# A one-core hybrid attention layer on Trainium2: opening loads cut in two, one more tile turned by VectorE, and a written order planned anew

## Chip, core and metric

The kernel runs on one core of one Trainium2 chip. The metric is the time of one execution in device microseconds (us), the median of several runs. A profiled execution has its own time and its own span, from the first to the last instruction.

## The reference, cut to what matters

One decoder layer on x of 2048 tokens by 1024 channels, all in float32:

```
h = rms_norm(x, norm_w);  proj = h @ w_in              # 1024 -> 2816 columns
rq, rk, rv, rg, sq, sk, sv, sg = split(proj)
ro = retention(rotary(rq), rotary(rk), rv)             # 4 heads, chunks of 128 tokens, a state carried on
ro = group_norm(ro) * ret_norm_w * silu(rg)
so = sliding_window_attention(sq, sk, sv, sinks, rel_bias) * silu(sg)   # 8 heads, window 128
return x + concat(ro, so) @ w_out                      # 1024 -> 1024
```

## The kernel before, in words

**Products.** The four large products (the projection in three groups of columns, 512, 384 and 512 wide, then the output projection, 512 wide) are made as Strassen products: seven products of blocks take the place of eight. For each of them, and for each of eight pairs of 128-token chunks, one product block is 12 matmuls of 512 (or 384) columns: 4 steps over the inner dimension, times 3 passes. The three passes are there because every float32 operand is split in a high part (`hi`, a rounded copy, made by ScalarE as a rule) and a low part (`lo`, the rest, made by VectorE): `xh*wh`, `xh*wl`, `xl*wh`. One group of columns has 56 such blocks.

**Small matmuls between them.** The sliding window needs 8 blocks `logits` (128 small matmuls each) and 8 blocks `values` (144 each); the retention needs 9 blocks `step` (up to 128 each); 16 single transposes turn keys (`turn k`). Of the 16 retention outputs that have been gated, those whose chunk is in `TURNED["gated"]` are turned by VectorE (a transpose of 32 by 32 blocks, a store to DRAM and four loads of 64 KB that put the blocks in place); the others take four transposes on TensorE and a copy by ScalarE. Before, 11 chunks are in the list and 5 are not (2, 7, 9, 12, 13).

**The order.** Every operation is entered into a `Program` with its engines and their costs, its buffers and a due time. `emit` then simulates the engines and writes the operations out, always the one that could start first by its costs, with the due time as tie-break and as the order of the queues. What it writes is the order of each engine on the chip; waits there are by semaphores. So a change of a due time (the tables `SHIFT` by label, `GROUPS` by label and stretch of 28 units, `SINGLE` by the operation's number) moves operations among others and changes no arithmetic. All plain loads and stores are issued by SyncE (SP) in one order.

**Instruction transfers.** TensorE's instructions are taken by the planner to come in pieces of 256 (`PIECE`), the next one asked for 320 instructions ahead (`ASKED`) and there `LONG` us later. An operation that would come to a border of pieces sooner is held back in the plan, so that others go first:

```
def late(o, s, occ):
    b, wait = border, 0.0
    while b <= place + o.many:
        a = b - ASKED
        at = s + (a - place) / o.many * occ if a >= place else asked.get(b, -LONG)
        wait = max(wait, at + LONG - s - (b - place) / o.many * occ)
        b += PIECE
    return wait
```

**The opening.** TensorE first runs ten warming matmuls on a constant. SP loads in turn a 256 KB tile of the first weights (`w`) and one of the first rows (`xfirst`, four chunks side by side), four of each. For inner step k=0, both 256-column halves of x are made high by ScalarE or VectorE, and w is scaled by the norm's weight and made high by ScalarE in one instruction (`part` with `split`). The first 48 matmuls go over the four chunks in turn, pass by pass for k below 3 (`products`, `passes`).

Of the kernel before, what the change touches and what calls it, by code (L numbers as in the profile page):

```python
# [40 lines left out]
NCH = S // P  # L41
# [22 lines left out]
SHARE = {"x": 25, "raw": 102, "acc": 73, "wr": 29, "wh": 16, "att": 27, "ret": 37, "rin": 87, "gate": 43, "mix": 73, "norm": 10, "res": 6, "turned": 3, "vn": 5, "first": 5, "block": 3, "rest": 6, "split": 53}  # L64

AHEAD_OF = {"x": 5.31, "wh": 14.22, "att": 30.46}

AHEAD, SPARE, SPARED = 13.889, 5, ("raw", "wr")

# [276 lines left out]
TURN = (1.9635, 2.7, 1.35)  # L346

GROUP = 28.0
GROUPS = {("scale k", 5): -0.35, ("load xk", 1): -0.74, ("mixed", 5): 0.86, ("load vn", 2): 1.11, ("load w", 0): 0.37}
SINGLE = {378: 2.98, 1033: 2.32, 910: -1.82, 395: 4.73, 18: -0.56, 25: 0.49, 394: -4.94, 1384: 4.33, 31: -0.91, 437: -1.09, 30: -2.54, 381: 2.45, 38: 0.49, 393: 0.51, 17: -0.02, 32: 0.37, 37: 4.06, 388: 2.37, 384: -1.41, 16: -1.27, 380: 0.9, 379: 3.45}  # L350

ACCUM = (1.25, 4.0, 0.1)

QUARTERS_IN = (1.05, 2.8, 1.6)

# [82 lines left out]
def layer(ctx, tc, xt, xfirst, xtok, nw, w_in, w_rn, qkw, sinks, biasg, rope, decays, dmask, gpow, w_out, out):  # L438
# [43 lines left out]
    def given(ap):  # L482
        return Buf(ap=ap)
# [42 lines left out]
    def f(t):  # L526
        return t.bitcast(F32)
# [61 lines left out]
    def split(raw, n, due, share, name, scale=None, quarters=False, labels=None):  # L589

        labels = labels or ("hi " + name, "lo " + name)
        hi, lo = kb(name, share, F32R), kb(name, share, F32R)
        of = (lambda t: t.rearrange("p (a k s) -> p k a s", a=4, s=32)) if quarters else (lambda t: t[:, :n])
        to = (lambda t: t.rearrange("p (k a s) -> p k a s", a=4, s=32)) if quarters else (lambda t: t[:, :n])
        if scale is None:
            op(
                {"A": act(n)}, lambda e: e.activation(to(hi()), of(raw()), AF.Copy), [raw], [hi], due,
                label=labels[0], also=(lo,),
            )
            op(  # L600
                both(n),
                lambda e: e.tensor_tensor(to(lo()), of(raw()), f(to(hi())), ALU.subtract),
                [raw, hi], [lo], due, label=labels[1],
            )
# [14 lines left out]
        return hi, lo  # L619
# [21 lines left out]
    def weights(src, c0, n, scale, base, seq):  # L641


        W = {m: [None] * 4 for m in range(1, 8)}
        at = {m: base + seq.first[m] for m in W}
        col, cols = scale

        def raw(q, i, due):
            t = kb("w", "wr")
            k, c = 4 * (q // 2) + i, c0 + q % 2 * n  # L650
            load(
                t, given(src[k * P : (k + 1) * P, c : c + n]), due - 3, n // 2, lambda t: t[:, :n],
                label="load first" if base == q == 0 else None,
            )
            return t

        def by(k):
            return (col, k) if k < cols else None

        def part(m, i, t, scale=None):  # L660
# [102 lines left out]
    def opening():  # L763

        made = []
        for k in range(KT // 2):
            t, hi, lo = kb("x", "raw"), kb("x", "x", F32R), kb("x", "x", F32R)

            load(t, given(xfirst[k]), -4.95 + 0.1 * k, label="load first")
            parts = []  # L770
            for i in range(2):
                c, due = slice(i * 256, (i + 1) * 256), -2.0 + 0.1 * k + 0.01 * i
                h, l = (Part(t, lambda t, c=c: t[:, c]) for t in (hi, lo))
                op(
                    {"A": act(256), "V": dve(256)} if k == 0 else {"A": act(256)},
                    lambda e, t=t, h=h, c=c: e.activation(h(), t()[:, c], AF.Copy) if e is A else e.tensor_copy(h(), t()[:, c]),
                    [t], [h], due, label="first hi", also=(hi, lo),
                )
                op(
                    both(256), lambda e, t=t, h=h, l=l, c=c: e.tensor_tensor(l(), t()[:, c], f(h()), ALU.subtract),  # L780
                    [t, h], [l], due, label="first lo", also=(hi, lo),
                )
                parts.append((h, l))
            made.append((hi, lo, parts))
        return made
# [4 lines left out]
    def products(B, W, n, base, seq, sink, plus=None, opening=None):  # L790
# [4 lines left out]
        def passes(m, acc, xh, xl, cols, k, d, goes_on, parts, which):  # L795


            wh, wl = W[m][k]
# [981 lines left out]
```

## Time and profile before

| | |
|---|---|
| median of 3 runs | 661.98 us (661.77 to 662.56) |
| the profiled execution's own time | 661.52 us |
| its span | 659.7 us |
| busy share: TensorE, VectorE, ScalarE, GpSimd | 99%, 87%, 71%, 7% |
| granted TensorE clock, mean | 0.999 |

In the profile PE is TensorE's matmuls, PEld its weight loads, DVE VectorE, ACT ScalarE, POOL GpSimd, SP SyncE; a q behind a name is that engine's sequencer. All instructions of this kernel have one line (434, a helper), so that groups are told apart by the tiles: `acc<-w,x` is a product block, `m<-ks,qT` logits, `m<-pT,vn` values, `m<-ident,ro` and `m<-ident,go` the turning of a gated tile. A row's busy time of matmuls is modelled at its end; the distance from one start to the next is the safer figure.

### The profile page before, as it was taken

The numbers are of one execution on the slowest core, as the hardware profiler recorded it, in microseconds if no ns is written. First come the engines' busy times: TensorE is split into PE (matmuls) and PEld (weight loads), VectorE is DVE, ScalarE is ACT, GpSimd is POOL, SyncE is SP. The second block draws the span as 40 slices with busy tenths as digits, with TensorE's granted clock in tenths as the row PEclk, the third lists the DMA queues.
The fourth block names the chain that finished last, engine by engine and source line by source line (L and its number), as shares of the span: only waits on it lengthen the run. The fifth ranks groups of instructions, "written<-read, shape, count | busy, mean of one in ns | idle before, by whom it ended". The sixth has DMA issues, their size and how long they took to land.

```text
span 659.7 us, 16248 instructions
## 1 busy us (share of the span) xinstructions
PE 654.7 (99%) x5930; PEld 561.2 (85%) x5930; DVE 574.0 (87%) x1328; ACT 469.1 (71%) x1141; POOL 43.5 (7%) x71
## 2 busy tenths in 40 slices
PE   9999999999999999999999999999999999999998
PEld 7888888888999999998888887888788888888886
DVE  5999987888689989899998999999999999974542
ACT  6774789667589778597999799898999765553000
POOL 0000000023300000000000000000000111133320
PEclk9999999999999999999999999999999999999999
DMA  9966399989598989999999989789999995179872
GB/s 317 386 231 239 112 327 313 320 264 325 122 237 259 255 232 275 342 300 302 278 233 275 259 272 289 211 268 245 260 287 257 181 284 135 40 138 205 192 160 97
DMA packets 152705, 160.34 MB, mean 243 GB/s; under 512 B 62000, under 2 KB 95152, under 8 KB 152624
## 3 DMA queue, kind: packets, MB, share of 16 engines
q1 hardware_dynamic: 147872, 150.90, 77.3%
q0 software_dynamic: 4608, 8.39, 8.1%
q8 instruction: 47, 0.77, 0.5%
q14 instruction: 34, 0.28, 0.1%
q10 hardware_dynamic: 144, 0.00, 0.0%
HBM read 97.32 MB, written 49.35 MB: 222 GB/s over the span
## 4 chain that ended last, share of the span: by engine, by line
PE 99%; issue 0%; DVE 0%; POOLq 0%
PE acc L434 88%; PE m L434 11%; DVE t L434 0%; POOLq L434 0%
## 5 line engine op out<-in xcount | busy, mean ns | idle before, releaser
L434 PE MATMUL acc<-w,x 128*128 128x512 f32 (+1 forms) x2700 | 586.5, 377 | 1.0 <-issue 1.0
L434 PEld LDWEIGHTS acc<-w,x 128*128 128x128 f32 x2700 | 493.9, 188 | 84.8 <-issue 4.8
L434 DVE TENSOR_TENSOR x<-x 128x512 fp32r<-128x512 f32 (+2 forms) x213 | 139.3, 681 | 11.5 <-ACT x L434 8.9
L434 ACT ACTIVATE x<-x 128x512 fp32r<-128x512 f32 (+1 forms) x180 | 106.7, 620 | 36.7 <-DVE x L434 16.4
L434 DVE TENSOR_TENSOR w<-w 128x512 fp32r<-128x512 f32 (+3 forms) x96 | 61.6, 666 | 3.9 <-ACT w L434 3.9
L434 ACT ACTIVATE lg<-lg,nm 128x160 f32<-128x160 f32 x128 | 53.0, 419 | 2.9 <-DVE nm L434 2.9
L434 DVE TENSOR_TENSOR s<-acc,s 128x512 f32<-128x512 f32 (+1 forms) x64 | 42.0, 657 | 13.8 <-PE acc L434 13.5
L434 DVE SCALAR_TENSOR_TENSOR w<-w,nw_sb 128x512 fp32r<-128x512 f32 (+3 forms) x72 | 49.8, 711 | 4.4 <-ACT w L434 3.0
L434 ACT ACTIVATE w<-w 128x512 fp32r<-128x512 f32 (+1 forms) x72 | 40.7, 603 | 13.0 <-DVE x L434 5.8
L434 DVE CUSTOM_DVE_ANT_0 lg<-m,bias,nsnk 128x160 f32<-128x160 f32 x128 | 39.8, 388 | 0.5 <-PE m L434 0.5
L434 DVE TENSOR_TENSOR t<-acc,t 128x512 f32<-128x512 f32 (+2 forms) x33 | 21.1, 640 | 17.0 <-PE acc L434 16.7
L434 DVE TENSOR_TENSOR r<-acc,t 128x512 f32<-128x512 f32 (+1 forms) x32 | 20.9, 653 | 13.5 <-PE acc L434 13.1
L434 POOL DMA_DIRECT2D c<-in_xtok x8 | 7.1, 890 | 371.9 <-ACT c L434 360.3
L434 ACT ACTIVATE w<-w,nw_sb 128x512 fp32r<-128x512 f32 (+3 forms) x42 | 27.3, 685 | 4.8 <-DMA w<-in_w_in 2.3
L434 ACT ACTIVATE c<-acc 128x512 f32<-128x512 f32 (+1 forms) x32 | 18.1, 567 | 13.9 <-PE acc L434 10.7
L434 ACT ACTIVATE s<-acc 128x512 f32<-128x512 f32 (+1 forms) x32 | 18.3, 573 | 13.3 <-PE acc L434 11.5
L434 DVE STREAM_TRANSPOSE pT<-lg 128x640 f32<-128x640 f32 x32 | 26.1, 838 | 0.9 <-ACT lg L434 0.7
L434 ACT ACTIVATE ro<-ro,nmu,rg 128x128 f32<-128x128 f32 x64 | 25.3, 489 | 1.1 <-DVE nmu L434 1.0
L434 DVE TENSOR_TENSOR t<-acc,s 128x512 f32<-128x512 f32 (+1 forms) x32 | 21.1, 658 | 4.6 <-PE acc L434 4.5
L434 ACT ACTIVATION_READ_ACCUMULATOR lg<-lg,nm 128x1 f32 x128 | 24.6, 192 | 0.0
L434 ACT ACTIVATE x<-go 128x512 fp32r<-128x512 f32 x26 | 16.1, 631 | 9.6 <-DVE x L434 3.1
L434 ACT ACTIVATE ro<-m 64x256 f32<-64x256 f32 (+2 forms) x52 | 20.6, 395 | 1.9 <-PE m L434 1.2
(147 smaller groups left out, 604.1 us busy)
## 6 DMA issues: line engine op xcount, KB each, us to landing
x<-in_xt SPq DMA_DIRECT2D x76, 256.0 KB, 4.9
planes_dram<-apart SPq DMA_DIRECT2D x48, 256.0 KB, 4.0
x<-s_dram SPq DMA_DIRECT2D x46, 256.0 KB, 4.5
w<-in_w_in SPq DMA_DIRECT2D x40, 256.0 KB, 5.2
xk<-in_xtok SPq DMA_DIRECT2D x32, 256.0 KB, 5.3
s_dram<-x SPq DMA_DIRECT2D x23, 256.0 KB, 4.2
w<-in_w_out SPq DMA_DIRECT2D x20, 256.0 KB, 4.1
vn<-aq_dram SPq DMA_DIRECT2D x8, 576.0 KB, 5.9
```

What stands on the lines that cost most here:

```text
L434: return lambda *a, **k: self.order.put(op(*a, **k))
```

## The change

It has four parts. (1) Opening: the first x tile (k=0) is loaded as two halves of 128 KB, each made high and low on its own. (2) Opening: the first weight tile's high part is made in two pieces, 192 columns by ScalarE and 320 by VectorE (`opened`); the matmuls of k=0 wait for both pieces. (3) Chunk 13 joins `TURNED["gated"]`: twelve tiles go by VectorE, four by TensorE (2, 7, 9, 12). (4) The planner's constants change, `LONG` from 5.5 to 8.0 among them, and the due times of some 190 groups and some 1,100 single operations: a new written order. `SHIFT`, `HELD` and the number of every other instruction stay.

```
-SHARE = {"x": 25, "raw": 102, "acc": 73, ... "gate": 43, "mix": 73, "res": 6, "vn": 5, ...}
-AHEAD_OF = {"x": 5.31, "wh": 14.22, "att": 30.46}
-AHEAD, SPARE, SPARED = 13.889, 5, ("raw", "wr")
+SHARE = {"x": 21, "raw": 70, "acc": 96, ... "gate": 20, "mix": 35, "res": 73, "vn": 49, ...}
+AHEAD_OF = {"x": 5.15, "wh": 44.79, "att": 26.63}
+AHEAD, SPARE, SPARED = 15.774, 5, ("raw", "wr")
...
-PIECE, FIRST, ASKED, LONG, MORE = 256, 193, 320, 5.5, 1.0125
-LATER, CROWD, MOST, SOONER = 1.586, -0.721, 2, 139.422
+PIECE, FIRST, ASKED, LONG, MORE = 256, 193, 320, 8.0, 1.0125
+LATER, CROWD, MOST, SOONER = 2.565, 0.719, 2, 156.112
...
-GROUPS = {("scale k", 5): -0.35, ...}            (5 entries)
-SINGLE = {378: 2.98, 1033: 2.32, ...}            (22 entries)
-ACCUM = (1.25, 4.0, 0.1)
+GROUPS = {("logits", 4): -10.19, ("hi x", 5): 1.84, ...}
+SINGLE = {..., 11: -424.48, ..., 15: -64.96, ..., 378: -99.66, ..., 379: -89.28, ..., 384: -79.0, ...}
+ACCUM = (1.7, 4.5, 0.1)
...
-TURNED = {"q": range(NCH), "qk": range(NCH), "gated": (0, 1, 3, 4, 5, 6, 8, 10, 11, 14, 15)}
+TURNED = {"q": range(NCH), "qk": range(NCH), "gated": (0, 1, 3, 4, 5, 6, 8, 10, 11, 13, 14, 15)}
...
+        def opened(t, scale):
+            b, k = scale
+            hi, lo = kb("w", "wh", F32R), kb("w", "wh", F32R)
+            pieces = []
+            for i, c in enumerate((slice(0, 192), slice(192, 512))):
+                h = Part(hi, lambda t, c=c: t[:, c])
+                m = c.stop - c.start
+                op(
+                    {"V": (0.13 + m / 1100, 0.2 + m / 1100, True)} if i else {"A": act(m, 0.09)},
+                    lambda e, h=h, c=c: e.activation(h(), t()[:, c], AF.Copy, scale=b()[:, k : k + 1])
+                    if e is A
+                    else e.tensor_scalar(h(), t()[:, c], b()[:, k : k + 1], None, op0=ALU.mult),
+                    [t, b], [h], -3.0, label="first hi", also=(hi, lo),
+                )
+                pieces.append(h)
...
         def part(m, i, t, scale=None):
+            if m == 1 and i == base == 0:
+                W[m][i] = opened(t, scale)
+                return
...
-            load(t, given(xfirst[k]), -4.95 + 0.1 * k, label="load first")
+            halves = [Part(t, lambda t, i=i: t[:, i * 256 : (i + 1) * 256]) for i in range(2)] if k == 0 else [t]
+            for i, b in enumerate(halves):
+                c = slice(i * 256, (i + 1) * 256) if k == 0 else slice(0, 512)
+                load(
+                    b, given(xfirst[k][:, c]), -4.95 + 0.1 * k + 0.01 * i, 256 // len(halves), label="load first", also=(t,)
+                )
...
-            pairs = ((parts[0], wh), (parts[0], wl), (parts[1], wh))
+            whole = pieces[0] if pieces else (wh,)
+            pairs = ((parts[0], *whole), (parts[0], wl), (parts[1], *whole))
```

Operations are numbered in the order in which they are entered. In the changed kernel number 11 is the load of the first weights, 15 that of the second, 378 and 379 are the two halves of the first x, 384 the second x. With their due times of -4.95 to -4.85 the entries of `SINGLE` put SP's loads in the order: first weights, first x in two halves, second x, second weights.

## Rows read from the trace of the kernel before

**Rows 1.** The page: busy us (share of the span) and instructions of each engine.

```profile
PE 654.7 (99%) x5930; PEld 561.2 (85%) x5930; DVE 574.0 (87%) x1328; ACT 469.1 (71%) x1141; POOL 43.5 (7%) x71
```

**Rows 2.** All waits of PE's product blocks, whole span: total us, times, longest us.

```profile
PE acc L434 <- issue: 1.0, 1, 1.0
```

**Rows 3.** Chain of work, 0 to 170 us: start, us, what, how many.

```profile
4.96 157.40 PE acc L434 x696
```

**Rows 4.** Timeline of PE, 388 to 403 us: start, length, instruction, count, idle before.

```profile
393.44 2.53 PE L434 MATMUL m<-pT,vn 32*64 32x128 f32 x144
395.90 0.73 PE L434 MATMUL acc<-w,x 128*128 128x512 f32 x2
397.59 3.92 PE L434 MATMUL acc<-w,x 128*128 128x512 f32 x16 [0.95 <-issue]
```

**Rows 5.** DMA queues: whole span, then 395.2 to 397.6 us (transfers, MB, share).

```profile
q8 instruction: 47, 0.77, 0.5%
...
q8 instruction: 1, 0.02, 2.7%
```

**Rows 6.** Timeline of PE, 502 to 507 us, start of the last group of products.

```profile
502.65 3.02 PE L434 MATMUL acc<-w,x 128*128 128x512 f32 x12
...
505.86 1.39 PE L434 MATMUL acc<-w,x 128*128 128x512 f32 x5
```

**Rows 7.** Timeline of VectorE, 531 to 533.4 us.

```profile
532.88 0.70 DVE L434 TENSOR_TENSOR x<-go,x 128x512 fp32r<-128x512 f32 x1
```

**Rows 8.** Stretches of all engines: length, then busy us (instructions) each, PEclk, DMA.

```profile
500.00:580.00 80.00, 80.00 (x357) 66.02 (x356) 80.00 (x134) 53.26 (x90) 9.73 (x11) 1.00 0.78 182
```

**Rows 9.** Timeline of PE, 220 to 232 us.

```profile
225.23 3.40 PE L434 MATMUL acc<-w,x 128*128 128x384 f32 x18
228.56 2.43 PE L434 MATMUL m<-ks,qT 64*32 64x160 f32 x128
```

**Rows 10.** Timeline of PE, 484.6 to 489 us: two gated tiles turned.

```profile
485.03 0.60 PE L434 MATMUL m<-ident,go 128*128 128x128 f32 x4
485.38 3.00 PE L434 MATMUL acc<-w,x 128*128 128x512 f32 x12
488.22 0.60 PE L434 MATMUL m<-ident,ro 128*128 128x128 f32 x4
```

**Rows 11.** A group of VectorE's instructions, 400 to 520 us: busy us, mean ns, idle before.

```profile
L434 DVE STREAM_TRANSPOSE g<-go 128x512 f32<-128x512 f32 x2 | 1.4, 710 | 0.0
```

**Rows 12.** Timelines of the opening: PE, then ScalarE, VectorE and SP's issues.

```profile
0.78 4.18 PE L434 MATMUL m<-const-float32-0.0 128*128 128x256 f32 x10 [0.78 <-PEq L1768]
4.78 0.80 PE L434 MATMUL acc<-w,x 128*128 128x512 f32 x1
5.37 0.63 PE L434 MATMUL acc<-w,x 128*128 128x512 f32 x1
5.79 0.63 PE L434 MATMUL acc<-w,x 128*128 128x512 f32 x1
7.72 0.85 PE L434 MATMUL acc<-w,x 128*128 128x512 f32 x3
...
3.69 0.72 ACT L434 ACTIVATE w<-w,nw_sb 128x512 fp32r<-128x512 f32 x1 [1.03 <-DMA w<-in_w_in]
4.32 0.40 ACT L434 ACTIVATE x<-x 128x256 fp32r<-128x256 f32 x1
5.99 0.72 ACT L434 ACTIVATE w<-w,nw_sb 128x512 fp32r<-128x512 f32 x1 [1.27 <-DMA w<-in_w_in]
6.64 0.73 ACT L434 ACTIVATE x<-x 128x256 fp32r<-128x256 f32 x2
...
4.29 0.29 DVE L434 CAST x<-x 128x256 fp32r<-128x256 f32 x1 [3.15 <-DMA x<-in_xfirst]
...
0.74 0.39 SPq L434 DMA_DIRECT2D w<-in_w_in  x1
1.19 0.44 SPq L434 DMA_DIRECT2D x<-in_xfirst  x1
```

More of the change, by code (lines that the diff above doesn't have):

```diff
@@ L62 @@
 SMALL, COUNTS = 3, {"ms": 1, "rxt": 1, "rqk0t": 1, "rqk1t": 1, "state": 7}
-SHARE = {"x": 25, "raw": 102, "acc": 73, "wr": 29, "wh": 16, "att": 27, "ret": 37, "rin": 87, "gate": 43, "mix": 73, "norm": 10, "res": 6, "turned": 3, "vn": 5, "first": 5, "block": 3, "rest": 6, "split": 53}
-AHEAD_OF = {"x": 5.31, "wh": 14.22, "att": 30.46}
-AHEAD, SPARE, SPARED = 13.889, 5, ("raw", "wr")
+SHARE = {"x": 21, "raw": 70, "acc": 96, "wr": 22, "wh": 17, "att": 49, "ret": 49, "rin": 106, "gate": 20, "mix": 35, "norm": 9, "res": 73, "turned": 2, "vn": 49, "first": 5, "block": 3, "rest": 6, "split": 57}
+AHEAD_OF = {"x": 5.15, "wh": 44.79, "att": 26.63}
+AHEAD, SPARE, SPARED = 15.774, 5, ("raw", "wr")
 STEPS = ((1, 2), (6,), (5,), (7, 4), (3,))
@@ L348 @@
 GROUP = 28.0
-GROUPS = {("scale k", 5): -0.35, ("load xk", 1): -0.74, ("mixed", 5): 0.86, ("load vn", 2): 1.11, ("load w", 0): 0.37}
-SINGLE = {378: 2.98, 1033: 2.32, 910: -1.82, 395: 4.73, 18: -0.56, 25: 0.49, 394: -4.94, 1384: 4.33, 31: -0.91, 437: -1.09, 30: -2.54, 381: 2.45, 38: 0.49, 393: 0.51, 17: -0.02, 32: 0.37, 37: 4.06, 388: 2.37, 384: -1.41, 16: -1.27, 380: 0.9, 379: 3.45}
-ACCUM = (1.25, 4.0, 0.1)
+GROUPS = {("logits", 4): -10.19, ("hi x", 5): 1.84, ("state", 5): 4.9, ("state", 4): -2.65, ("stats", 4): 4.55, ("so", 4): 3.62, ("lo x", 6): 1.51, ("sum go", 6): 1.59, ("lo x", 2): -5.66, ("turn k", 2): -5.07, ("lo w", 5): -0.99, ("lo x", 3): -3.1, ("store apart", 6): -4.58, ("rotary", 5): 4.29, ("load go", 5): -4.6, ("first lo", -1): -19.79, ("store x", 1): 2.46, ("sum w", 1): 3.58, ("scale k", 4): 1.12, ("qn", 4): 1.98, ("gate", 6): -2.77, ("load aq", 2): 5.2, ("more", 6): 2.56, ("kn", 2): 8.85, ("turn weights", 3): 1.58, ("lo x", 1): -1.23, ("rsqrt", 4): -7.08, ("lo w", 4): -3.52, ("load w", 0): -0.75, ("store c", 0): 2.69, ("sum x", 6): -1.51, ("load g", 5): -3.95, ("sum ro", 6): 7.54, ("hi x", 2): 0.77, ("first hi", -1): -9.06, ("step", 5): -3.01, ("load x", 1): -6.84, ("load go", 6): 1.47, ("hi w", 7): 4.0, ("store t", 2): -3.32, ("load x", 3): 3.4, ("lo w", 0): -6.05, ("add s", 4): -5.32, ("load w", 2): -1.6, ("load w", 6): 0.9, ("lo x", 0): -3.81, ("lo w", 1): -1.16, ("turn gated", 5): 3.02, ("turn by dma", 4): 2.75, ("ks", 4): -1.6, ("store so", 3): -0.28, ("lo x", 7): -3.0, ("add s", 0): 3.17, ("load akv", 3): -5.08, ("scale first", 0): 7.96, ("store ro", 4): -4.83, ("step", 4): 0.51, ("add r", 5): -1.58, ("group norm", 5): 2.5, ("load w", 1): 3.16, ("load bias", 1): -1.31, ("load turned", 5): 1.55, ("store s", 2): -3.8, ("sum w", 3): 3.84, ("load x", 2): -1.72, ("apart", 2): 7.72, ("load aq", 4): 1.55, ("add s", 5): -1.0, ("store r", 1): 2.21, ("copy s", 1): -8.15, ("hi w", 2): -1.22, ("copy s", 5): -3.36, ("store apart", 4): -7.07, ("sum qk", 0): -0.46, ("bias", 4): -4.52, ("decay", 5): -0.86, ("hi w", 3): 4.68, ("sum w", 4): -0.13, ("turn gated", 4): 3.58, ("scale w", 6): -2.3, ("so", 3): -9.26, ("hi x", 4): 0.03, ("store s", 7): -9.11, ("scale w", 1): -1.35, ("load go", 4): -6.61, ("add t", 7): -4.12, ("gate", 4): 9.25, ("scale w", 3): 1.57, ("load ", 5): -0.89, ("load turned", 6): -0.34, ("store s", 3): 0.6, ("load snk", 0): 4.79, ("exp", 4): 0.76, ("bias", 2): 4.15, ("hi x", 3): 0.38, ("exp sink", 3): 5.29, ("store s", 1): 4.94, ("square qk", 0): -0.59, ("scale w", 5): -5.23, ("add t", 6): -0.81, ("sum x", 0): -0.14, ("gate", 5): 3.23, ("add r", 4): -1.63, ("base", 4): -2.87, ("store s", 6): -0.66, ("ks", 2): -2.03, ("exp sink", 2): -4.19, ("store ro", 5): -5.31, ("lo w", 2): -2.41, ("mixed", 4): -0.77, ("sum w", 2): 0.47, ("ro", 4): -5.02, ("qn", 3): -3.35, ("rsqrt", 2): 3.17, ("exp", 3): 0.43, ("hi w", 5): 2.17, ("qn", 2): -1.31, ("base", 5): 1.43, ("copy s", 2): 3.65, ("rsqrt", 5): -2.58, ("apart", 5): -0.29, ("bias", 3): 1.74, ("turn weights", 2): 1.24, ("store c", 4): -0.26, ("square x", 1): -1.42, ("apart", 3): -0.6, ("sink", 2): 3.16, ("more", 5): -3.16, ("table", -1): 1.25, ("hi x", 1): -0.43, ("bias", 1): 4.76, ("add s", 6): -0.76, ("load xk", 0): -0.46, ("lo w", 3): -1.88, ("load first", -1): -2.04, ("turn gated", 6): 4.05, ("store so", 4): -6.87, ("turn by dma", 2): 3.11, ("sum w", 5): -3.08, ("sink", 3): -1.08, ("add t", 3): 1.45, ("copy s", 0): 6.6, ("denominator", 3): -0.35, ("turn by dma", 1): -2.4, ("store ", 7): 4.64, ("no values", 0): -0.79, ("normalise", 4): -1.46, ("store g", 5): 3.06, ("lo w", 6): -1.26, ("store t", 4): 1.52, ("add t", 8): 0.81, ("load turned", 4): -1.78, ("store apart", 5): 0.82, ("", 1): -1.94, ("sum w", 7): -3.5, ("logits", 3): -0.02, ("add t", 0): 1.77, ("copy c", 1): 0.15, ("add s", 2): 0.74, ("load x", 5): 0.07, ("values", 3): 0.25, ("lo x", 5): -0.05, ("load vn", 3): -1.19, ("silu", 6): -0.34, ("", 2): -3.4, ("sum qk", 1): -0.7, ("load w", 3): -1.66, ("decay", 4): 0.48, ("load vn", 4): -0.9, ("add r", 1): -2.09, ("mixed", 5): -0.78, ("mixed", 6): -2.73, ("add s", 3): -1.38, ("store t", 7): -0.36, ("kn", 3): 0.2, ("add s", 7): -0.4, ("store c", 6): -2.8, ("scale w", 4): -1.31, ("apart", 1): -2.98, ("square qk", 1): 0.62, ("copy c", 6): -0.77, ("store apart", 2): 0.38, ("exp", 2): 1.03, ("load dec", 0): 1.69, ("more", 7): -0.18, ("load w", 5): -0.52, ("square x", 0): 1.46, ("add r", 6): -0.48, ("store s", 5): 0.25, ("load g", 4): 0.7, ("hi w", 0): 0.5, ("nothing", -1): 0.85, ("silu", 4): -0.66, ("store apart", 1): 0.55, ("load akv", 1): -3.14, ("add r", 0): 1.55, ("add t", 1): 0.29, ("hi w", 1): 1.53, ("load x", 4): -0.01, ("scale w", 2): 1.64, ("denominator", 4): -1.27, ("square qk", 2): -1.63, ("scale v", 1): -0.66, ("ro", 5): -3.0, ("factors", 4): -1.2, ("load akv", 2): -0.11, ("load aq", 3): -0.15, ("exp sink", 4): -1.1, ("copy s", 4): -0.35, ("load ", 3): 2.22, ("store so", 2): 2.04, ("sum w", 6): -1.47, ("copy c", 3): 1.54, ("load w", 4): -3.13, ("store c", 5): 1.15, ("values", 2): -2.07, ("group norm", 4): -1.93, ("store c", 2): -0.29, ("turn weights", 4): -0.46, ("load g", 6): -1.23, ("scale v", 2): 0.32}
@@ L658, in by @@
             return (col, k) if k < cols else None
+        def opened(t, scale):
[13 more added lines that the diff above has]
+                pieces.append(h)
+            op(
+                {"V": (0.13 + n / 960, 0.21 + n / 960, True)},
+                lambda e: e.scalar_tensor_tensor(
+                    lo(), t(), b()[:, k : k + 1], f(hi()), op0=ALU.mult, op1=ALU.subtract
+                ),
+                [t, b, *pieces], [lo], -1.9, label="first lo", also=(hi,),
+            )
+            return hi, lo, pieces
         def part(m, i, t, scale=None):
+            if m == 1 and i == base == 0:
+                W[m][i] = opened(t, scale)
+                return
             W[m][i] = split(
@@ L767, in opening @@
             t, hi, lo = kb("x", "raw"), kb("x", "x", F32R), kb("x", "x", F32R)
-            load(t, given(xfirst[k]), -4.95 + 0.1 * k, label="load first")
+            halves = [Part(t, lambda t, i=i: t[:, i * 256 : (i + 1) * 256]) for i in range(2)] if k == 0 else [t]
[3 more added lines that the diff above has]
+                    b, given(xfirst[k][:, c]), -4.95 + 0.1 * k + 0.01 * i, 256 // len(halves), label="load first", also=(t,)
+                )
             parts = []
@@ L772, in opening @@
                 c, due = slice(i * 256, (i + 1) * 256), -2.0 + 0.1 * k + 0.01 * i
+                b = halves[i % len(halves)]
                 h, l = (Part(t, lambda t, c=c: t[:, c]) for t in (hi, lo))
                 op(
-                    {"A": act(256), "V": dve(256)} if k == 0 else {"A": act(256)},
+                    {"A": act(256), "V": (0.07 + 256 / 1100, 0.13 + 256 / 1100, True)} if k == 0 else {"A": act(256)},
                     lambda e, t=t, h=h, c=c: e.activation(h(), t()[:, c], AF.Copy) if e is A else e.tensor_copy(h(), t()[:, c]),
-                    [t], [h], due, label="first hi", also=(hi, lo),
+                    [b], [h], due, label="first hi", also=(hi, lo, t),
                 )
@@ L780, in opening @@
                     both(256), lambda e, t=t, h=h, l=l, c=c: e.tensor_tensor(l(), t()[:, c], f(h()), ALU.subtract),
-                    [t, h], [l], due, label="first lo", also=(hi, lo),
+                    [b, h], [l], due, label="first lo", also=(hi, lo, t),
                 )
@@ L795, in passes @@
         def passes(m, acc, xh, xl, cols, k, d, goes_on, parts, which):
-            wh, wl = W[m][k]
+            wh, wl, *pieces = W[m][k]
             def go(e):
```

1 line of the change is left out of this document (added).

## The prediction, as it was written before the result was known

> **What bounds the kernel now.** I read the page first. TensorE is busy 99% of the span [rows 1], so the other engines matter only where they make it wait. The list of PE's waits comes next: in 660 us its product blocks waited once, 1.0 us, with "issue" as releaser, so for nothing that the profile shows [rows 2]. Everything else is the matmuls' own pace: the chain has 696 of 512 columns in 157.40 us, 0.226 us each [rows 3]. A change can therefore take time out only in five ways: that one wait, the work of PE itself, the opening, the tail, or waits hidden between pipelined matmuls. The tail (a small add and its store) isn't touched.
>
> The timeline shows the wait: two matmuls start at 395.90, the next at 397.59 [rows 4]. Two take 0.45 us, so 1.69 - 0.45 = 1.24 us are lost. Right before stands a `values` block: 144 matmuls in 2.46 us, each with a weight load, 288 instructions. Queue q8 moved 47 instruction transfers, 0.77 MB in all, 16 KB each; 47 for 2 x 5930 matmuls and loads is one for some 250 instructions, and one of them ran in the 2.4 us around the wait [rows 1, 5]. That fits an engine which came to the end of its instructions. It isn't proof; it is the step that I weigh most below.
>
> Last I read where waits would come from. The last group of products has 56 blocks; its first starts at 502.65, the second at 505.86, later ones 12 x 0.226 = 2.71 us apart [rows 3, 6]. The twelfth so starts near 533.0 and needs its low part of x at its third matmul, at 533.5. Taking VectorE's low parts in the order of the blocks, that one runs from 532.88 to 533.58 [rows 7]: no slack is left. VectorE has no idle time from 500 to 580: 134 instructions in 80 us, 0.60 us apiece [rows 8]. So PE is the bound, but VectorE stands right behind it there.
>
> **The change part by part.**
>
> *The longer transfers.* The plan before asks 320 instructions ahead and allows 5.5 us. Counted back from the wait: 2 matmuls (4 instructions), the block (288), 14 matmuls before it (28). They were asked for 14 x 0.226 = 3.17 us before 393.44, at 390.3; PE got there at 396.35, 6.1 us later, and went on at 397.59, after 7.3 us. The plan thought 5.5 enough and it wasn't; 8.0 covers 7.3. If that is the cause, 1.24 us go. The transfers themselves don't get faster: the new plan only has to keep more large matmuls between blocks of small ones, which are there to be had. Bounds: 0 (another cause, or such a wait elsewhere) to -1.24; I take -1.24. What speaks for another wait elsewhere: these times vary. Two other small blocks lie only 18 matmuls apart, from 225.23 to 228.56 [rows 9]; at the pace of the block above (2.46 us for 288), 320 instructions there are 3.33 + 284 x 2.46/288 = 5.8 us, and PE didn't wait. The Trainium skill, page "Runtime: NRT & Kernel Launch", section "Instruction fetch mechanics", says that instructions come in blocks of 256 while the current ones run, and that this is mostly hidden, since the sequencer dispatches more slowly than the fetch fills. By that rule part of the change would be for nothing (first rival). Block size and trace agree; on hiding, the trace has this one place against it.
>
> *The twelfth tile.* A tile turned by PE costs it 485.38 - 485.03 = 0.35 us, and the following 12 matmuls take 488.22 - 485.38 = 2.84 where 2.71 is their pace, 0.13 more [rows 3, 10]: 0.48 us, off PE's path for one tile. In return VectorE gets a transpose of 0.71 us [rows 11], and SP five issues (one store, four loads), some 0.45 us each by the start distance of its first two [rows 12], 2.2 us in all. Later loads queue behind these, but no product block waited for a load in the whole span [rows 2]. Chunk 13 is wanted in the thirteenth block of the last group, near 536, and PE turned the last of its tiles before 505.86 [rows 6]: 30 us cover the detour through DRAM. If that cover is gone, PE waits for it at once, up to the 2.2 us of issues. For VectorE the cover is only other work that can wait: at 0.60 us a piece in the full stretch [rows 8], the cost is 0 (something else goes later) to 0.60 (all ahead of the twelfth block). I take 0 and keep 0.60 for the range.
>
> *The opening.* The first product starts at 4.78, when the ten warming matmuls are through; its weight load isn't ahead of it, so 0.59 us pass to the second, then 0.42 to the third [rows 12]. 0.42 us for 512 columns is half the later pace, the 1.2 GHz level of the clock. In the new opening the weights' high part is ready at about 4.1 instead of 4.41: ScalarE's 192 columns take under the 0.40 of its 256-column row, VectorE's 320 between the 0.29 of its 256-column copy and twice that. The first half of x lands between the first weights (3.69) and now (4.29) and is high after 0.29 to 0.40: 4.0 to 4.7. Both fall under the cover of the warming matmuls, which end at 4.78 whatever is loaded. So the start can't move; only 0.59 - 0.42 = 0.17 us can go, and not all at this level, if the faster clock comes at a fixed moment. Against it: SP issues one load more, 0.45 us, and the second weights go behind the second x, one landing of 6.64 - 5.99 = 0.65 us later. Their high part is then ready at 5.99 + 0.65 + 0.45 + 0.72 = 7.81; step k=1 begins at 7.72 + 2 x 0.226 = 8.17 and, moved up, at 8.0. That holds by 0.2 us; if one more transfer of 0.65 goes ahead of it, 0.45 us are lost. Bounds -0.17 to +0.45; I take -0.10.
>
> *The new orders.* All matmuls of the products and small blocks stay. Before, PE waited for nothing but the one above, so a new order has almost nothing to take back beyond the terms named (0.1 us at the twelfth block), and can add waits anywhere. I take 0, from -0.4 to some us.
>
> Sum: -1.24 - 0.48 - 0.10 = -1.82 us. The profiled execution took 661.52 us (span 659.7 and 1.8 around it), so it becomes 659.7. The runs' median lies 0.46 above the profiled time; kept, 661.98 - 1.82 = 660.16.
>
> **The rivals.**
>
> First: the wait isn't one for instructions, or another comes in its place. Then 0.48 + 0.10 are left: 661.4. For it: the profile shows nothing that was waited for, and the transfers vary. The skill's page above speaks for it too. Against it: 7.3 us is well beyond what the old plan allowed, right behind the densest block, with a transfer under way. 0.12.
>
> Second: VectorE gives back the gain at the start of the last group. The twelfth block has no slack, and each of its instructions put ahead of that point is 0.60 us of PE's time. With one to three: 660.8 to 662.0. 0.14.
>
> Third, slower: the same place, decided by the spacing. If `logits`, `values` and `step` blocks must stay farther apart, the last of them come later, their outputs are gated later, and more of VectorE's work falls into the full stretch before 533. Above 663.3 it needs 3.14 us beyond the forecast, 3.14/0.60, so six instructions or more; with seven it is 664.4. For it: four us in a chain of 500 are little. Against it: several sums of weights in this stretch belong to product 6, whose first block is the seventeenth, and can wait. 0.13.
>
> Fourth: less than forecast. Small blocks end up side by side (0.13 us less for each), or the runs above the profiled time held a second such wait: below 659.4. 0.08.
>
> **How the numbers follow.** My forecast gets 0.53; its own range is 659.4 to 660.65. Some 0.2% of 662, 1.3 us, is what a measurement of this kernel can tell from no change, so faster means below 660.66, slower above 663.3. Faster: 0.53 + 0.08 = 0.61. Same: 0.12 + 0.14 = 0.26. Slower: 0.13. The range for 8 in 10 leaves out nearly all of the third rival and the far end of the fourth: 659.2 to 662.8.
>
> **What would show it.** Right: PE's list of waits without a wait for "issue", and the last stretch of matmuls over 1.8 us sooner; sixteen instead of twenty transposes of gated tiles on PE; the second product 0.42 behind the first, and no gap at the twelfth matmul; about as many q8 transfers as now. Wrong: a gap of about 1 us with "issue" behind some block of small matmuls (first rival); PE waiting for DVE near 530 (second and third); PE waiting for ScalarE or a load near 8 us (opening). The prediction fails as a whole if the new order puts short waits in many places, too small for one row but seen in the pace of the 512-column matmuls.

## The result and the profile after

| | before | after |
|---|---|---|
| median of the runs | 661.71 us (660.34 to 664.25, 22 runs) | 664.51 us (662.06 to 668.07, 22 runs) |
| ratio, 95% interval | | 1.0039 [1.0024, 1.0053] |
| profiled execution, its span | 661.52 us, 659.7 us | 662.82 us, 661.0 us |

The change makes the kernel slower, by more than the 0.2% that can be told from no change; the forecast was 660.2, with a range from 659.2 to 662.8. The profiled execution of after is one of its faster ones, so its trace can explain 1.3 us of the 2.8 between the medians; the rest has to come from the experiments.

The page of after, busy us of each engine and, from its part on queues, the instruction transfers; they answer to [rows 1] and [rows 5]:

```profile
PE 654.1 (99%) x5926; PEld 560.3 (85%) x5926; DVE 573.0 (87%) x1328; ACT 466.4 (71%) x1140; POOL 43.5 (7%) x71
...
q8 instruction: 46, 0.75, 0.5%
```

All waits of TensorE (not of the product blocks alone), total us, times, longest us; they answer to [rows 2]:

```profile
PE m L434 <- issue: 0.9, 1, 0.9
PE m L434 <- PEq L1802: 0.8, 1, 0.8
PE m L434 <- DVE nm L434: 0.7, 1, 0.7
PE acc L434 <- ACT x L434: 0.5, 1, 0.5
```

The second is the start of the program, as long before. Three are new, and the one of 1.0 us in [rows 2] is gone. The first of them, in the timeline of TensorE from 190 to 200 us (start, length, instruction, count, idle before):

```profile
191.07 2.31 PE L434 MATMUL m<-pT,vn 32*64 32x128 f32 x129
194.27 0.48 PE L434 MATMUL m<-pT,vn 32*64 32x128 f32 x15 [0.89 <-issue]
194.67 3.91 PE L434 MATMUL acc<-w,x 128*128 128x384 f32 x21
```

This is a `values` block, 15 matmuls before its end: 3.60 us from its start to the next block, where the one in [rows 4] takes 2.46. It looks like the wait of [rows 4] once more, 203 us earlier: same releaser, same sort of block, nearly the same size. The runs below test that.

The wait for `nm`, in the timeline of TensorE around 280 us and in the chain that ends there (start, us, what):

```profile
279.69 1.84 PE L434 MATMUL acc<-w,x 128*128 128x384 f32 x9
282.26 0.30 PE L434 MATMUL m<-ident,kn 128*128 128x128 f32 x1 [0.73 <-DVE nm L434]
```

```profile
270.39 6.31 DMA x<-s_dram
...
276.76 2.35 DMA rq_dram<-r
...
282.10 0.02 DVE nm L434
```

VectorE's `nm` is only the last link. By the profile the chain comes from SyncE, which issues the store `rq_dram<-r` only when the load of 270.39 has landed, eight issues earlier on its queue, after 6.31 us. The trace's issue records name the semaphore of each transfer: SyncE's take eight in turn, so the ninth waits for the first.

The opening, timelines of TensorE, ScalarE and VectorE, and the chain of the third matmul of the products; they answer to [rows 12]:

```profile
5.45 2.92 PE L434 MATMUL acc<-w,x 128*128 128x512 f32 x10 [0.50 <-ACT x L434]
...
3.35 1.28 ACT L434 ACT_TABLE_LOAD   x1 [3.35 <-DMA nw_sb<-in_nw]
4.64 0.45 ACT L434 ACTIVATE w<-w,nw_sb 128x192 fp32r<-128x192 f32 x1
5.00 0.40 ACT L434 ACTIVATE x<-x 128x256 fp32r<-128x256 f32 x1
5.78 0.42 ACT L434 ACTIVATE x<-x 128x256 fp32r<-128x256 f32 x1 [0.38 <-DMA x<-in_xfirst]
...
3.61 0.39 DVE L434 TENSOR_SCALAR w<-w,nw_sb 128x320 fp32r<-128x320 f32 x1 [3.61 <-DMA w<-in_w_in]
```

```profile
1.68 4.08 DMA x<-in_xfirst
5.76 0.02 issue
5.78 0.43 ACT x L434
6.21 0.04 issue
6.25 1.89 PE acc L434 x7
```

ScalarE's table load, 1.28 us, now stands in front of its first useful instruction; before, it ran from 1.16 to 2.44 while the first loads were under way (timeline of ScalarE, the kernel before):

```profile
1.16 1.28 ACT L434 ACT_TABLE_LOAD   x1 [1.16 <-PEq L1768]
```

(Before, the planner had put a memset and a one-column activation early, and the table came with that. With a new due time both come at 83 us; the planner knows of no table.) The Trainium skill, page "ScalarE: Activation LUTs", section "What ACT_TABLE_LOAD costs", gives some 1283 ns for a load; the row agrees. And the second half of x lands at 1.68 + 4.08 = 5.76, where before the whole tile was there at 4.29 [rows 12]. The cut makes the second half the third transfer on SyncE's queue. In the six traces with x in two halves it lands between 5.33 and 5.88; in the six with x whole and nothing put behind it, the third transfer, there the second weights, lands between 5.17 and 6.11. So by these traces it is the place on the queue that is late, not this tile.

The gated tiles turned by TensorE, all instructions on tile `m` by form (count: shortest, median, longest ns, first and last start):

```profile
L434 PE MATMUL m<-ident,ro x12: 270/272/273, 411.1 to 525.8; 128*128 128x128 f32 x12
...
L434 PE MATMUL m<-ident,go x4: 272/272/273, 481.4 to 481.8; 128*128 128x128 f32 x4
```

Last the end: SyncE's waits from 653 us on, first in after, then in e5, a run described below:

```profile
SPq L1810 <- DMA out<-t: 1.1, 1, 1.1
```

```profile
SPq L1781 <- DMA out<-t: 0.3, 1, 0.3
```

The rows of the semaphore instructions themselves say why. At the end SyncE waits for its eight semaphores in the order of their numbers:

```
after (672 transfers): last store issued 657.68, on semaphore 100
  passed: 100 at 659.28, 102 659.34, 103 659.43, 104 659.51, 105 659.58, 106 659.65, 107 660.04, 108 660.12
e5    (671 transfers): last store issued 655.29, on semaphore 109
  passed: 100 at 656.12, 103 656.20, 104 656.26, 105 656.33, 106 656.39, 107 656.45, 108 656.51, 109 656.89
```

From issue to its own semaphore the last store takes 1.60 us in both. With 671 transfers it stands last in the list, and the others are passed while it is under way; with 672 it stands first, and 0.84 us of passing come after it. From the start of the last matmul to the end of the span it is 3.47 us before (666 transfers; five semaphores come after its own), 3.99 after, 3.13 to 3.14 in the three usable traces with 671.

The ledger of the two profiled executions, by starts of matmuls:

| place | before | after | difference |
|---|---|---|---|
| 690th product matmul starts (opening) | 160.98 | 161.26 | +0.28 |
| stall behind `values` at 396 | 1.24 | 0 | -1.24 |
| `values` at 191 | 2.46 (any) | 3.60 | +1.14 |
| `values` at 239 | 2.46 (any) | 2.56 | +0.10 |
| nine product matmuls ahead of 282 | 1.56 (without a wait) | 2.57 | +1.01 |
| `turn k` at 337 | 0.03 (any) | 0.36 | +0.33 |
| gated transposes: 20 in five groups, 16 in three | 1.77 + 5 x 0.13 | 1.50 + 3 x 0.13 | -0.53 |
| last matmul to end | 3.47 | 3.99 | +0.52 |

The sum is +1.61; the spans differ by 1.3. Of the 0.3 that after gains elsewhere, 0.11 is a short wait of before at 533.6 that after doesn't have, and 0.09 is one change fewer between small matmuls and products; the rest lies in many small pieces. The +0.10 at 239 is a border of two instruction transfers as well (landed 240.29, TensorE on at 241.57; see the table of landings below). Of the +1.01 at 282, 0.23 are there in e2 too (1.79), and so is all of the +0.33 at 337.

### The profile page after: what moved, and what is told of

Read it like the earlier page. It is cut to its first block, busy times and chain, and to the rows that moved or that the text cites. A ratio compares the mean times of both kernels' runs of the same rounds, so it can differ in the third digit from the quotient of the medians.

```text
span 661.0 us, 16187 instructions
## 1 busy us (share of the span) xinstructions
PE 654.1 (99%) x5926; PEld 560.3 (85%) x5926; DVE 573.0 (87%) x1328; ACT 466.4 (71%) x1140; POOL 43.5 (7%) x71
## 4 chain that ended last, share of the span: by engine, by line
PE 96%; DMA 2%; issue 0%; ACT 0%; DVE 0%; SPq 0%; POOLq 0%
PE acc L434 86%; PE m L434 10%; DMA x<-s_dram 1%; DMA x<-in_xfirst 1%; DMA rq_dram<-r 0%; SPq L434 0%; ACT x L434 0%; ACT w L434 0%; DVE x L434 0%; DVE lg L434 0%; DVE t L434 0%; DVE nm L434 0%; POOLq L434 0%
## 5 line engine op out<-in xcount | busy, mean ns | idle before, releaser
L434 ACT ACTIVATE w<-w,nw_sb 128x512 fp32r<-128x512 f32 (+4 forms) x41 | 26.3, 674 | 3.7 <-PE acc L434 3.1
L434 PE MATMUL m<-pT,vn 32*64 32x128 f32 (+1 forms) x1152 | 20.6, 285 | 0.9 <-issue 0.9
```

What stands on the lines that cost most here:

```text
L434: return lambda *a, **k: self.order.put(op(*a, **k))
```

## The experiments

In all kernels called forced, each engine's order is written out instead of planned, so that a part can be edited and the rest stays:

```
+            forced, by = self.ops[ORDER[done][0]], ORDER[done][1]
-            for e, found in avail.items():
+            for e, found in ((by, [(forced.due, forced.n, forced)]),):
```

**First four: which part costs?**

**e1_table_early.** After's order, forced, with the table brought in at once:

```
-    load(nw_sb, given(nw), -9, 4, cost=BESIDE)
+    def first(e):
+        e.dma_start(nw_sb(), nw)
+        e.activation(once(), zero, AF.Copy)
+    op(BESIDE, first, [given(nw)], [nw_sb], -9, label="load nw_sb")
```

> The changed kernel with its written order kept operation by operation, but ScalarE's one-column activation that brings its table stands again right behind the load of the norm's weights. Theory O (the loss sits in the opening, where the table load of 1.28 us now stands in front of the first weights): TensorE's first product at 4.8 to 5.0 us instead of 5.45, and 0.5 to 1.5 us of the 2.8 come back, so 0.15 to 0.3% over the kernel before. Theory W (the new written order waits in many places later): 0.3 us at most, 0.35 to 0.4% over before.

663.18 us, ratio 1.0018 [1.0004, 1.0032]. The first product matmul starts at 4.61, but the third at 6.17: it waits for the second half of x, as in after. The 20th starts at 10.48, in after at 10.26, so in this pair of traces the earlier table brings nothing (though the full clock came at 6.86 here and at 5.33 in after); in the medians it is 1.3 us, with intervals of the ratios that overlap. What the table alone costs stays open.

**e2_body.** Everything of after behind the opening (order, `LONG`, twelfth tile), forced, with the opening before: x whole, w by ScalarE alone, the old order of the first loads. The table early as in e1.

```
-                W[m][i] = opened(t, scale)
...
-            halves = [Part(t, ...) for i in range(2)] if k == 0 else [t]
+            load(t, given(xfirst[k]), -4.95 + 0.1 * k, label="load first")
```

> The changed kernel's written order and its twelfth tile, with the opening of the kernel before (whole first rows, first weights by ScalarE alone, loads in the old order, table early). Theory O: as fast as before or faster, 0 to -1 us (the twelfth tile's 0.48 us and the steadier transfers remain). Theory W: 1.5 to 2.8 us slower than before, with a spread of runs as wide as that of the changed kernel (6 us).

661.59 us, ratio 0.9991 [0.9978, 1.0004]. So what after loses comes in with the opening; but the body alone gains next to nothing, where two terms of the prediction's sum stood. Its trace says why, TensorE from 190 to 200 us:

```profile
191.39 2.31 PE L434 MATMUL m<-pT,vn 32*64 32x128 f32 x129
194.63 0.47 PE L434 MATMUL m<-pT,vn 32*64 32x128 f32 x15 [0.93 <-issue]
```

The same stall as in after, at the same matmul, 1.18 us. The wait for `nm` isn't there, though the nine product matmuls ahead of that place take 0.23 us more than without a wait (see the ledger).

**e3_open.** The order before, forced, with the new opening's code (halves, `opened`), the table early: the diff of e2 the other way.

> The kernel before, its written order kept, with the new opening alone: first rows in halves, first weights' high part on two engines, table early, loads in the old turn with one more among them. Theory O: 0.5 to 2 us slower, the second half of the rows landing over 1 us after 4.29. Theory W: within 0.3 us of before. The forecast's term for it was -0.10 us.

663.14 us, ratio 1.0011 [0.9995, 1.0027], by itself not to be told from no change. The 20th product matmul starts at 10.45 instead of 10.00, the stall of 396 is there (1.1 us), and a new one named "issue" of 0.6 stands in a `values` block at 244, which has none before.

**e4_long8.** The kernel before with one number changed, planned anew:

```
-PIECE, FIRST, ASKED, LONG, MORE = 256, 193, 320, 5.5, 1.0125
+PIECE, FIRST, ASKED, LONG, MORE = 256, 193, 320, 8.0, 1.0125
```

> The kernel before with the allowance of an instruction transfer at 8.0 instead of 5.5 and nothing else changed, so that the planner writes a new order from the old due times. If the transfers were the cause of the 1.24 us wait and a longer allowance avoids it: 1.2 us faster, no wait for issue in the list. If any new order brings its own waits (theory W): 0 to 3 us slower, and a wider spread.

668.65 us, ratio 1.0099 [1.0080, 1.0118]. TensorE's waits:

```profile
PE acc L434 <- DVE w L434: 2.0, 1, 2.0
PE acc L434 <- DVE r L434: 1.8, 1, 1.8
PE m L434 <- issue: 1.4, 1, 1.4
```

With the old due times, the wider spacing makes VectorE late, and it doesn't even keep off the instruction wait: at 404 us a block landed 9.1 us after it was asked for, more than the 8.0 allowed. It says nothing of after's due times, which go with 8.0.

**Next four: is it the instruction blocks, and what in the opening?** From each trace I counted TensorE's weight loads, matmuls and semaphore instructions in order, took the border of each transfer (the first instruction that comes with it) from the planner's own numbers (193 + 256 n, asked 320 ahead), and compared with the time at which that transfer landed on q8:

| kernel | asked | landed | TensorE goes on | later by |
|---|---|---|---|---|
| before | 390.40 | 396.31 | 397.59 | 1.28 |
| after | 185.61 | 192.88 | 194.27 | 1.39 |
| e1 | 185.81 | 193.61 | 195.02 | 1.41 |
| e2 | 186.10 | 193.18 | 194.63 | 1.45 |

Each wait named "issue" stands at a border and ends 1.3 to 1.5 us after the landing. In e2, with the stall taken out, the stretch from asking to that border is 7.3 us by starts (7.6 by the row's 0.93) and another, at 241.8, 6.8: less than the plan's 8.0. One cause can be counted: the plan takes 1.0125 instructions for each load and matmul, and up to 193.6 us the trace has 2,229 of these and 11 semaphore instructions, so the plan is 17 too far. With 24 more instructions ahead of everything, every stretch in e2 would be 8.1 us or more. That can be had without touching the order, by cutting the warming matmuls smaller.

**e5_body_ahead24.** e2 with that edit:

```
-WARM = (256, 256, 256, 256, 128)
+WARM = (128,) * 7 + (64,) * 4
```

> The kernel of e2_body (the new order of the work, the old opening) with one edit: the ten warming matmul instructions pairs at the start are cut into smaller pieces, the same columns in all, so that 24 more TensorE instructions stand ahead of everything else. Every border between two blocks of 256 instructions then falls 24 instructions earlier in the work; order and work are the same. From the trace of e2_body, the stretch from the instruction at which a block is asked for (320 ahead) to the border, its own stall taken out, is 7.6 us at 193.7 and 6.8 us at its shortest; with the borders 24 earlier it is 8.1 us at its shortest and over 8.6 at 193. Theory I (the waits named issue are instruction blocks that land late, and where the borders fall decides who waits): the wait of 0.9 us inside the values at 193 goes, none as long comes elsewhere, values take 2.46 us instead of 3.64, TensorE ends 0.9 to 1.2 us earlier, ratio to before 0.9970 to 0.9985. Rival W (the wait belongs to that place's operands or to chance): 0.9 us or more stays there or elsewhere, ratio as of e2_body, 0.9978 to 1.0004, middle 0.9991.

659.57 us, ratio 0.9972 [0.9961, 0.9984]: faster than both kernels. TensorE's waits are the start alone, and the block at 191 is whole:

```profile
PE m L434 <- PEq L1773: 0.8, 1, 0.8
```

```profile
190.48 2.53 PE L434 MATMUL m<-pT,vn 32*64 32x128 f32 x144
192.94 3.91 PE L434 MATMUL acc<-w,x 128*128 128x384 f32 x21
```

A short stall is left at 240 (0.5 us over all `values`, 20.20 for 8 x 2.46): that block landed 7.5 us after it was asked for, TensorE went on 1.49 later. The list of waits doesn't name it.

**e6_before_ahead24.** The kernel before, order forced, with the same edit.

> The kernel before, every engine in its order, with the warming matmuls cut as in e5_body_ahead24: 24 more TensorE instructions ahead, all borders 24 earlier in the work. In the trace of before the stretch from asking to the border at 396.6 us is 6.2 us without its stall, and it stalled 1.0 to 1.24; with the borders 24 earlier it is 7.6 us there, and the shortest stretches are 5.8 us at 352, 229 and 210, where the kernel before has 5.7 to 5.8 and doesn't stall. Theory I: the wait of 1.0 us at 396 goes or falls under 0.2, TensorE ends about 1 us earlier, ratio 0.998 (0.9970 to 0.9990). Rival W (the wait of the kernel before was not an instruction block, or another comes in its place at once): a wait of about 1 us is still in the list, ratio 0.9995 to 1.0010.

664.54 us, ratio 1.0041 [1.0024, 1.0058]: the expectation of a gain was wrong. TensorE's waits, and three stretches of its trace (length, busy us and instructions of each engine, PEclk, DMA share, GB/s):

```profile
PE m L434 <- issue: 1.8, 1, 1.8
PE acc L434 <- issue: 1.7, 1, 1.7
```

```profile
397.30:400.40 3.10, 1.34 (x30) 0.83 (x15) 3.10 (x9) 3.10 (x10) 0.00 (x0) 1.00 0.93 301
400.40:403.90 3.50, 3.50 (x10) 2.77 (x9) 1.58 (x4) 3.50 (x14) 0.00 (x0) 0.51 1.09 176
403.90:408.00 4.10, 4.10 (x21) 3.35 (x20) 3.58 (x7) 3.77 (x12) 0.00 (x0) 1.00 1.08 388
```

Both waits are blocks again: landed at 212.54 and 397.92, 7.2 and 8.8 us after they were asked for, TensorE on at 214.03 and 399.35, 1.49 and 1.43 later. What I had left out is that the landing moves too. And behind the second wait the clock stood at half: 10 product matmuls in 3.50 us where the next row has 21 in 4.10.

**e7_body_halves.** e2 with the x tile of k=0 in halves, w whole. The edit brings back after's code of the opening and switches `opened` off in it:

```
-            if m == 1 and i == base == 0:
+            if m == 1 and i == base == 9:
```

> The kernel of e2_body with one part of the new opening: the first x tile is loaded in two halves, one behind the other on the queue; the first weights stay whole on ScalarE, the order of the other first loads is the old one. Theory O1 (the halves are what the opening loses by): the second half lands at about 5.7 to 5.9 us instead of the whole tile's 4.3, the second and third product wait for it, the 20th product starts 0.4 to 0.8 us later than in e2_body at the same clock, ratio 0.0007 to 0.0015 above that of e2_body, so 0.9998 to 1.0006. Rival O2 (the pieces of the weights and the order of the loads cost it, or what was lost lies behind the opening altogether): as e2_body, 0.9991 within 0.0010, and the 20th product within 0.2 us of it.

663.70 us, ratio 1.0037 [1.0021, 1.0053]: the halves alone bring nearly all the loss, but not where I had put it. The 20th product matmul starts at 9.98, in e2 at 9.97, with the full clock a good microsecond sooner here. The waits:

```profile
PE m L434 <- issue: 1.2, 1, 1.2
PE m L434 <- PEq L1807: 0.8, 1, 0.8
PE m L434 <- DVE nm L434: 0.7, 1, 0.7
```

And the tail is 3.9 us instead of 3.13: 672 transfers instead of 671.

**e8_body_opened.** e2 with w in two pieces, x whole; after's code again, with the halves switched off:

```
-            halves = [Part(...) ...] if k == 0 else [t]
+            halves = [Part(...) ...] if k == 9 else [t]
```

> The kernel of e2_body with the other part of the new opening: the high part of the first weights in two pieces, 192 columns by ScalarE and 320 by VectorE; the first x tile is loaded whole. Theory O1: x still lands at 4.3 us and its first half is ready at about 4.75, so the first product starts within 0.1 us of e2_body's 4.79 and nothing is gained; VectorE's piece, 0.39 us, is over before x lands; the 20th product within 0.1 us, ratio 0.9991 within 0.0010. Rival O2 (the pieces cost): the low part of the weights or of x comes later on VectorE and the 20th product starts 0.3 us or more later, ratio 0.9998 or more.

661.41 us, ratio 1.0000 [0.9987, 1.0013], neither side shown. Its profiled execution took 2,002 us and its trace isn't used.

**Last four: one transfer more, and the change with its borders moved.**

**e9_body24_twin.** e5 with one small transfer more that nobody reads:

```
+                def two(e, t=t):
+                    e.dma_start(t(), xfirst[0])
+                    e.dma_start(twin(), nw)
```

> The kernel of e5_body_ahead24 with one transfer more on SyncE's queue: behind the first x tile, whole, a second copy of the small weights column (4 numbers a row) that nobody reads. 672 transfers on that queue instead of 671, as in after and e7_body_halves. In the traces so far the transfers of the queue take eight semaphores in turn, and at the end SyncE waits through all of them one behind the other, 0.06 to 0.39 us each: with 671 transfers the last output is on the last of the list (e2, e5), with 672 on the first (after, e1, e7), and SyncE goes through the others after it has landed. Theory T (one transfer more costs at the end): from the last TensorE matmul to the end of the span 3.9 to 4.0 us instead of 3.14, ratio to before 0.9972 plus 0.0012, so 0.9978 to 0.9990. Rival H (what the halves cost has to do with the halves alone): the tail stays at 3.1 to 3.2 us, ratio as of e5, 0.9961 to 0.9984.

660.42 us, ratio 0.9986 [0.9973, 0.9999]. The last store is on semaphore 100, the first in the list, passed at 656.99; the others go to 657.42, 0.43 us. The tail is 3.62 us: 0.48 over e5, half of what I expected, since the one slow step of the list (0.39 us in after) falls ahead of the landing here. By the trace the mechanism holds, with 0.4 to 0.85 us; the intervals of this ratio and e5's overlap.

**e10_after_ahead24.** The changed kernel itself, order forced, with e5's edit.

> The changed kernel, every engine in its order, with the warming matmuls cut into smaller pieces as in e5_body_ahead24, 24 TensorE instructions more ahead of everything. Theory I (the wait of 0.9 us inside the values at 193 is an instruction block, and where the borders fall decides it): the wait goes or falls under 0.5, values take 20.2 us in all instead of 20.9, the wait for nm at 282 (0.7) and the tail of 3.9 us stay; ratio 1.0039 less 0.0011 to 0.0018, so 1.0018 to 1.0032. Rival W: as after, 1.0024 to 1.0053, a wait named issue of 0.9 us or more somewhere.

662.42 us, ratio 1.0008 [0.9992, 1.0023], 2.1 us less than after. Each engine does the same instructions in the same order in both traces, but for the warming matmuls. Its waits:

```profile
PE acc L434 <- ACT x L434: 0.4, 1, 0.4
PE acc L434 <- DVE x L434: 0.2, 1, 0.2
```

The stall at 193 is gone, and with it the wait for `nm`, against expectation. There the chain's load took 6.2 to 6.4 us in after, e1 and e7, 5.5 in e2, and 4.6 to 5.2 in the four kernels without the stall.

**e11_body24_halves.** e7 with e5's edit.

> The kernel of e5_body_ahead24 with the first x tile loaded in two halves and nothing else. Theory T alone (the halves cost as one transfer more at the end): tail 3.9 to 4.0 us, no wait for nm at 282, ratio 0.9984, as e9_body24_twin. Theory T and V (with the halves the transfer of vn at 270 takes 6.0 to 6.2 us instead of 5.0 to 5.3, and its chain makes TensorE wait 0.7 to 0.8 us at 282 for nm, as in after, e1 and e7): that wait too, ratio 0.9995. Rival N (the difference of e7 and e2 was chance): as e5, 0.9972 within 0.0012, tail 3.1.

661.35 us, ratio 0.9994 [0.9979, 1.0010]. No `nm`, so the wait at 282 isn't the halves' own. Against e5 its last matmul starts 1.17 us later: 0.5 in the opening and 1.3 from 427 to 434 and near 480 us, where its list names 0.2 for VectorE, less the 0.6 that e5 loses at 240 and 335. The tail is 3.56 us, 0.4 longer.

**e12_before_tile13.** The kernel before with the twelfth tile alone, planned with the old due times:

```
-TURNED = {..., "gated": (0, 1, 3, 4, 5, 6, 8, 10, 11, 14, 15)}
+TURNED = {..., "gated": (0, 1, 3, 4, 5, 6, 8, 10, 11, 13, 14, 15)}
```

> The kernel before with tile 13 of the gated stage turned by VectorE as well, twelve tiles, and nothing else of the change; the planner plans with the old due times, so some VectorE and SyncE work stands in another place. Theory G (four TensorE transposes less, each 0.089 us from one start to the next, and VectorE has room): 16 transposes take 1.50 us instead of 1.77, ratio 0.9992 to 0.9998 (0.27 to 0.48 us less), the wait of 1.0 us at 396 stays. Rival (VectorE or a moved border between instruction blocks gives it back): ratio 1.0000 or more, with a wait for VectorE past 480 us or one named issue at another place than 396.

661.46 us, ratio 1.0002 [0.9988, 1.0016]. The transposes take 1.42 us instead of 1.77, the stall of 396 stays (1.46), and TensorE waits for VectorE where the prediction saw no slack:

```profile
533.94 0.73 PE L434 MATMUL acc<-w,x 128*128 128x512 f32 x2 [0.22 <-ACT x L434]
535.34 1.88 PE L434 MATMUL acc<-w,x 128*128 128x512 f32 x7 [0.66 <-DVE x L434]
```

That is the second rival's place, in a plan with the old due times. After has no such wait: its new order keeps VectorE in time there.

## Why the prediction was wrong

*The longer transfers, -1.24.* The mechanism was right: the wait was an instruction block that came late, as the table of landings and e5 show, and in after it is gone from 396. The step that failed is "8.0 covers 7.3": that the new plan keeps enough large matmuls between small blocks everywhere. At 193 the stretch was 7.5 us without the stall, not 8.0. The block landed 7.3 us after it was asked for and TensorE went on 1.39 later, after 8.66 us, so a full 8.0 wouldn't have covered it either. So +1.14 came back, which is the first rival ("or another comes in its place"), to which I gave 0.12. I had used the one landing of the kernel before as if it were a constant; asked to landed goes from 2.1 to 12.0 us in these traces. The Trainium skill, page "Runtime: NRT & Kernel Launch", section "Instruction fetch mechanics", calls the cost at a border of 256 instructions mostly hidden; most of the 45 or so borders of each trace agree, but 10 of 13 usable traces have one or two that cost 0.3 to 1.8 us.

*The tail.* "The tail isn't touched" is the second step that failed. No operation of the tail changed, but the number of transfers did: a store and four loads for the twelfth tile and one half of x bring 666 to 672, and the place of the last store among eight semaphores with it. +0.52, against a sum that had 0. By the trace 671 would have made it -0.33.

*The opening, -0.10 with bounds -0.17 to +0.45.* +0.28: inside the bounds, for other reasons, and with the full clock from 5.33 us instead of 6.45, which no edit earned; at one clock the loss isn't measured. "Both fall under the cover of the warming matmuls" failed twice. I costed the two instructions that make the first high parts and not the table load that their engine needs first (it sat at 1.16 in the opening before, ahead of all rows that I read), and I gave the first half a landing without asking for the second's, 5.76, in the queue's third place.

*The twelfth tile, -0.48.* -0.53 in the ledger. Right, VectorE's part at nothing included; e12 shows that it doesn't hold with the old due times.

*The new orders, 0* (the tables have 221 groups and 1,480 single operations, not some 190 and 1,100). +1.01 at 282 and +0.33 at 337: the "waits anywhere" of that term, each about a microsecond or below. At 282 it isn't the order alone: e2 and the four kernels with moved borders have the same order there and lose at most 0.23.

Of the signs that the prediction named, sixteen transposes, as many q8 transfers (46) and no gap at the twelfth matmul of the opening came out, and the pace of the 512-column matmuls stayed at 0.227. The list without "issue" didn't, the second product matmul came 0.34 behind the first and not 0.42, and the last matmul starts 0.78 us later than before, not 1.8 sooner. The wait that was named as the sign of the first rival is there.

With the terms as they came the ledger and the spans give +1.3 and not -1.82. The other 1.5 us of the difference between the medians no trace of after shows. e10 says where to look: moving the borders alone takes 2.1 us off the median, but 1.1 off the span of the profiled executions, where 2.4 are gained at 193, 239, 282 and 337, 0.4 are lost before 70 us and 1.0 between 427 and 482. The same stall was 1.69 us in e1. That its size varies from run to run, and that this is the rest, is argued, not shown. Why the load at 270 lands later behind the stall stays open.

## What to carry to other kernels

Count what a change adds to each queue and each engine's instruction stream, not only what it computes: one transfer or a few instructions more move every later border and semaphore, here worth 0.5 us (the tail of e9) to 2.1 us (e10). Where a wait has no releaser in the profile, line up the instruction transfers' landings with it; if they match, try the same order with the borders moved by some instructions (0.3% here, the best kernel of this study), and expect a new place to be hit in another order (+0.4% in e6). Before an early instruction that looks idle is moved, see whether a table load comes with it.

## What the runs showed of the hardware

- TensorE went on 1.28 to 1.56 us after the late block had landed, in all 10 traces that have such a wait (9 in the list of waits, and e5).
- At the end of the program, SyncE's pass through eight semaphores costs 0.06 to 0.39 us each; with 671, 672 and 666 transfers the last matmul is followed by 3.13 to 3.14, 3.56 to 3.99 and 3.45 to 3.48 us.
- Behind a wait of 1.76 us in e6, and of 2.0 us in e4, the granted clock fell to half (0.51 in e6's stretch above); behind the waits of 0.9 to 1.7 us it stayed full, and behind another wait in e4, of 1.83 us, too.
- The clock reached its full level between 3.7 and 6.9 us in different executions, with warming matmuls from 0.78 in all of them: in before 0.43 us between product matmuls ahead of it, 0.23 after. The kernel before, e4 and e12 have the same instructions in the opening; in them the 20th product matmul starts at 10.00, 9.28 and 10.07, with the full clock from 6.45, 4.14 and 6.57: 0.8 us that no kernel had earned.
